# Moving both attention score blocks one gate tile later in a fused decoder layer

## The chip, the cores and the metric

The kernel runs on one core of one Trainium2 chip. The metric is the device time of one execution in microseconds. A core has a matrix engine (TensorE, "PE" in the profile), a vector engine (VectorE, "DVE"), a scalar engine (ScalarE, "ACT"), a general engine (GpSimd, "POOL") and a sync engine (SyncE, "SP") whose queue issues nearly all transfers here. Each engine takes its own instructions strictly in the order of the program, and waits where an operand isn't there yet.

## The reference

The layer maps x (256 tokens, 1024 features, float32) to an output of the same shape:

```
h = rmsnorm(x);  q, k, v, u_pool, gate_logits = split(h @ w_in)
q, k = rotary(rmsnorm(q)), rotary(rmsnorm(k))          # 8 heads of 64
attn = softmax(causal(q k^T / 8)) v
pooled = per-group map of (trailing mean over 2, 4, 8, 16 tokens - u_pool)
gates = sigmoid(gate_logits + b_gate)                  # 2 x 1024
x = x + (gates0 * (attn @ w_branch_attn) + gates1 * (pooled @ w_branch_pool)) @ w_out
up = conv3(rmsnorm(x) @ w_up)
out = x + (silu(up_gate) * up_value) @ w_down
```

With 256 tokens and blocks of 256, the block-sparse attention of the reference is plain causal attention over one block.

## The kernel before

Every product of two float32 matrices is made of three matmuls on split operands: a high part rounded on ACT (`high`, L91), a low part, the remainder, on DVE (`low`, L95 and L97), and then high x high, high x low and low x high on PE (`mm3`, L103 to L105). All weights come in blocks of 1 MB: a load on SP's queue (L132, tiles `raw_*`), then two halves of `high` (`hi_*`) and `low` (`lo_*`). A raw buffer is loaded again as soon as the low part of the block that was in it has been made, so the place of a load on SP's queue follows from the place of a `low` on DVE's queue.

The order of work is written out in the program. After q, k, v and the four pool groups come the 16 gate tiles, n = 0 to 15 (L649 to L681). A gate tile is 24 matmuls `ps_g<-xhi/xlo,hi_g/lo_g`; `chunk("g")` takes a new weight block at every even n. Between the tiles other work is placed by n: the last steps on the heads' q and k (`part_high`, `part_low`, which write tiles `qp` and `kp`), the scores, and at n = 12 the pool maps (`pool_maps`, PSUM tile `ps_m`), whose results are scaled two tick calls later by `pool_scaled` (`poolh` on ACT, `pooll` on DVE L97). `tick()` counts the tiles, and `later(m, f)` puts f after m more ticks.

The heads are dealt with in four pairs, two pairs at a time. For one such half `scores` makes 20 matmuls (L534) into the PSUM tiles `ps_s` of its two pairs (the pool `ps2` has two such buffers, and `ps_m` and the later `ps_o` use the same two). Then DVE adds the mask and takes the row maxima (L542 to L549), and ACT makes the exponentials (L562): those of the first pair at once, those of the second (`behind`) after the next gate tile. Then a block transposition on DVE (L280) and a store to HBM (`spill`, L284, `home_w<-y`) turn the weights of a pair; one tick after that four reads (`fill`, L292, `sm` or `y<-home_w`) bring them back. At the last pair the row sums go the same way: `home_sums` (L583, four small stores) and the broadcast reads `RS<-home_sums` (L590). The first pair's transposition is put down two ticks after its exponentials, that of the second goes through the list `held`, and is emitted at the end of a tile, after `ahead` has put down the next pieces of weight splitting.

After the 16 gate tiles comes the pool branch, eight feature blocks j (`ps_bp`, 12 matmuls each); with j = 4 the attention values of all pairs (`ps_o`, L600, 32 matmuls) are inserted. They are scaled by RS (L616), and split into the tile `heads` (ACT L91, DVE L95). The attention branch `ps_ba` follows with eight blocks, which need `heads`; then the output projection and the FFN, which take the rest of the time.

Of the kernel before, what the change touches and what calls it, by code (L numbers as in the profile page):

```python
# [70 lines left out]
def hybrid_layer_kernel(ctx: ExitStack, tc: tile.TileContext, xq_d, xtok_d, par_d, wkv_d, wpg_d,  # L71
# [70 lines left out]
    for c, (name, src) in enumerate(order):  # L142
        n = CH if name == "q" else src.shape[-1]
# [17 lines left out]
    def next_high():  # L161
        if at[0] < len(pieces):
            c, sl, first, _ = pieces[at[0]]
            if c - oldest() >= WBUFS:
                return
            at[0] += 1
            if first:
                moving = order[c][0] in "qkv"
                place = MOVING if moving else 0
                his[c] = whi_p.tile([P, CH + P], F32R, tag="whi", name=f"hi_{order[c][0]}{c}")[:, place:]  # L170
                place = MOVING if moving else FAR
                los[c] = wlo_p.tile([P, CH + P], F32R, tag="wlo", name=f"lo_{order[c][0]}{c}")[:, place:]
            high(his[c][:, sl], raw(c, sl))

    def next_low(eager=False):
        if at[1] < at[0] - STAGGER or at[0] == len(pieces) > at[1] or (at[1] < at[0] and eager):
            c, sl, _, last = pieces[at[1]]
            at[1] += 1
            low(los[c][:, sl], his[c][:, sl], raw(c, sl))
            if last:  # L180
                split.add(c)
                while loaded[0] - RAWBUFS in split and order[loaded[0] - RAWBUFS][0] != "q" and loaded[0] < len(order):
                    load()
# [3 lines left out]
    def ahead(upto=0):  # L187

        next_high()
        next_low()  # L190
        if at[1] - sum(p[0] < used[0] for p in pieces) < upto:
            next_high()
            next_low()

    def chunk(name):
        c = used[0]
        used[0] += 1
        spent.update(i for i in range(c) if order[i][0] != "dn")
        assert order[c][0] == name and all(p[0] != c or name == "dn" and p[3] for p in pieces[at[1]:]), (name, order[c][0])
        return his[c], los[c]  # L200
# [130 lines left out]
    def big(name):  # L331
        return tmp.tile([P, 2 * 2 * 3 * P], F32, tag="big", bufs=2, name=name)
# [90 lines left out]
    def tick():  # L423
        clock[0] += 1
        for fn, args in due.pop(clock[0], []):
            fn(*args)


    def feature_tile(w, c, name):
        hi, lo = w  # L430
        ps = bank(f"ps_{name}")
        for k in range(KD):
            sl = slice(k * 256 + c * P, k * 256 + (c + 1) * P)
            mm3(ps[:, 0:S], (hi[:, sl], lo[:, sl]), (xhi[:, k, :], xlo[:, k, :]), k == 0, k == KD - 1)
        return ps
# [61 lines left out]
    def part_high(name):  # L497
        for t in range(NT):
            high(part(name, 0, t), head_rows(name, t))

    def part_low(name):
        for t in range(NT):
            low(part(name, 1, t), part(name, 0, t), head_rows(name, t))
# [3 lines left out]
    def gate(n):  # L507
        return gates[:, n // 2, n % 2, :]
# [9 lines left out]
    def scores(hps):  # L518
        if not turned:
            sms, ys = big("sm0"), big("y0")  # L520
            turned.append(ys)
        else:
            sms = turned.pop()
            ys = act.tile([P, 2 * 2 * 3 * P], F32, tag="qk", name="y2")
        pss = []
        for hp in hps:
            pss.append(ps2.tile([P, 2, 512], F32, tag="ps2", name=f"ps_s{hp}"))
            for t, part, keys in ((1, 1, 0), (1, 0, 0), (1, 0, 1), (0, 0, None), (0, 1, 0)):
                for j in range(2):
                    rows = slice(j * DH, (j + 1) * DH)  # L530
                    out = pss[-1][:, j, TOK[t]]
                    if keys is None:
                        out = pss[-1][:, j, :].rearrange("p (a b) -> p a b", b=P)[:, 0:4:3, :]
                    nc.tensor.matmul(out, qp[rows, part, hp, t * P:(t + 1) * P],  # L534
                                     kp[rows, :, hp, 0:P] if keys is None else kp[rows, keys, hp, 0:(t + 1) * P],
                                     start=t == part == 1, stop=(t, part, keys) in ((1, 0, 1), (0, 1, 0)),
                                     skip_group_check=True)
        for i, (hp, ps) in enumerate(zip(hps, pss)):
            on = slice(i * 6 * P, (i + 1) * 6 * P)
            sm = sms[:, on].rearrange("p (j c) -> p j c", j=2)  # L540
            mx = tmp.tile([P, 2, 2], F32, tag="mx", name=f"mx{hp}")
            nc.vector.tensor_tensor(sm[:, :, TOK[0]], ps[:, :, 3 * P:4 * P],  # L542
                                    mask[:, 1:2, :].to_broadcast([P, 2, P]), ALU.add)
            for j in range(2):
                for t in (1, 0):
                    nc.vector.tensor_tensor_reduce(sm[:, j, TOK[t]], ps[:, j, TOK[t]],
                                                   whole if t else sm[:, j, TOK[0]], 1.0, LOWEST,
                                                   ALU.add, ALU.max, mx[:, t, j:j + 1])
            nc.vector.scalar_tensor_tensor(mx, mx, -1.0, qs[:, :, 2 * hp:2 * hp + 2], ALU.mult, ALU.mult)  # L549
            if i == 0:  # L550
                exponentials(hp, sm, mx, ys[:, on], sms[:, on])
            else:
                behind.append((exponentials, hp, sm, mx, ys[:, on], sms[:, on]))
# [4 lines left out]
    def exponentials(hp, sm, mx, *flat):  # L558
        for j in range(2):
            for t in (1, 0):  # L560
                at = j * H + NT * hp + t
                nc.scalar.activation(sm[:, j, TOK[t]], sm[:, j, TOK[t]], AF.Exp, bias=mx[:, t, j:j + 1],  # L562
                                     scale=qs[:, t, 2 * hp + j:2 * hp + j + 1], accum_out=rsum[:, at:at + 1])
        if hp % 2:
            later(1, held.append, (turn_weights, hp, *flat))
        else:
            later(2, turn_weights, hp, *flat)
# [57 lines left out]
    def sigmoids(n):  # L625
        for _ in range(min(n, len(waiting))):
            f = waiting.pop(0)
            nc.scalar.activation(gate(f), gate(f), AF.Sigmoid, bias=par[:, C_BG + f:C_BG + f + 1])

    def pool_maps():  # L630
        wph, wpl = chunk("pool")
        pm = ps2.tile([P, 2, 512], F32, tag="ps2", name="ps_m")
        for g in range(NG):
            sl = slice(g * P, (g + 1) * P)
            mm3(pm[:, g // 2, (g % 2) * S:(g % 2 + 1) * S], (wph[:, sl], wpl[:, sl]),
                (poolh[:, g, :], pooll[:, g, :]), True, True)
        for i in range(2):
            later(1 + i, pool_scaled, pm, (2 * i, 2 * i + 1))
# [10 lines left out]
    for n in range(2 * KD):  # L649
        if n == 1:  # L650
            for _ in range(2):
                next_high()
            for _ in range(2):
                next_low()
        if n in (2, 3):
            part_high("q" if n == 2 else "k")
        if n in (5, 10):
            scores((0, 1) if n == 5 else (2, 3))
        if n == 2 * MAPS:
            pool_maps()  # L660
            ahead()
        b, c = n // 2, n % 2
        if c == 0:
            w = chunk("g")
        ps = feature_tile(w, c, f"g{n}")
        tick()
        ahead(AHEAD if n % 2 else 0)
        for fn, *args in behind + held:
            fn(*args)
        behind.clear()  # L670
        held.clear()
        f = 2 * GATES[b] + c
        if n in PLAIN:
            nc.scalar.activation(gate(f), ps[:, 0:S], AF.Copy)
            plain.append(f)
        else:
            nc.vector.tensor_tensor(gate(f), ps[:, 0:S], R1, ALU.mult)
        if n in (2, 3):
            part_low("q" if n == 2 else "k")
        if n >= 2 * KD - 2:  # L680
            sigmoids(3)  # L681
# [295 lines left out]
```

## Time and profile before

| | us |
|---|---|
| median of three runs (lowest, highest) | 331.68 (329.95, 332.16) |
| the profiled execution, its own time | 329.45 |
| its span in the trace | 327.7 |
| PE busy in the span | 322.5 (98%) |
| DVE busy | 259.5 (79%) |
| ACT busy | 201.4 (61%) |
| first scores start on PE | 62.5 |
| second scores start on PE | 78.83 |
| attention values start on PE | 104.89 |
| attention branch starts on PE | 111.84 |

Times in the rows count from the start of the span. A row of the timeline has the start, the duration, the engine, the line, the operation and what it writes and reads; in brackets stands how long the engine sat idle just before it, and what ended that. Durations of neighbouring instructions overlap, since the engines are pipelined: what a step costs its engine is the difference between two starts. SPq rows are the issues on SP's queue, not the transfers; "DMA to landing" is the time from an issue until the data has landed.

### The profile page before, as it was taken

The numbers are of one execution on the slowest core, as the hardware profiler recorded it, in microseconds if no ns is written. First come the engines' busy times: TensorE is split into PE (matmuls) and PEld (weight loads), VectorE is DVE, ScalarE is ACT, GpSimd is POOL, SyncE is SP. The second block draws the span as 40 slices with busy tenths as digits, with TensorE's granted clock in tenths as the row PEclk, the third lists the DMA queues.
The fourth block names the chain that finished last, engine by engine and source line by source line (L and its number), as shares of the span: only waits on it lengthen the run. The fifth ranks groups of instructions, "written<-read, shape, count | busy, mean of one in ns | idle before, by whom it ended". The sixth has DMA issues, their size and how long they took to land.

```text
span 327.7 us, 6762 instructions
## 1 busy us (share of the span) xinstructions
PE 322.5 (98%) x2708; PEld 315.5 (96%) x2708; DVE 259.5 (79%) x447; ACT 201.4 (61%) x329; POOL 71.3 (22%) x89
## 2 busy tenths in 40 slices
PE   8999999899999999999999999999999999999996
PEld 8888899899999999999999999999999999999995
DVE  5839989998989866879997978686868686868844
ACT  5768609584995657668676746474647474746520
POOL 1006690000000051130421222212121212121330
PEclk9999999999999999999999999999999999999999
DMA  7999799748977933644627455454545454643003
GB/s 257 424 418 233 240 356 304 281 180 254 301 251 225 403 128 120 241 157 144 242 80 307 158 228 196 190 202 187 199 187 206 181 210 176 212 174 130 0 2 128
DMA packets 15710, 69.72 MB, mean 213 GB/s; under 512 B 2112, under 2 KB 6464, under 8 KB 8640
## 3 DMA queue, kind: packets, MB, share of 16 engines
q1 hardware_dynamic: 15264, 69.17, 59.6%
q8 instruction: 21, 0.34, 0.4%
q10 hardware_dynamic: 416, 0.13, 0.3%
q14 instruction: 9, 0.07, 0.1%
HBM read 65.61 MB, written 3.68 MB: 211 GB/s over the span
## 4 chain that ended last, share of the span: by engine, by line
PE 80%; DMA 12%; DVE 5%; issue 1%; ACT 1%; SPq 1%; DVEq 0%; ACTq 0%
PE ps_up L104 12%; PE ps_up L105 12%; PE ps_up L103 12%; PE ps_d L838 6%; PE ps_d L839 6%; PE ps_d L837 6%; DMA raw_v<-in_wkv 4%; PE ps_g L103 3%; PE ps_g L104 3%; PE ps_g L105 3%; DMA R<-rows 3%; PE ps_out L105 2%; PE ps_out L104 2%; PE ps_out L103 2%; DMA xq<-in_xq 2%; DMA home_k<-y_k 1%
## 5 line engine op out<-in xcount | busy, mean ns | idle before, releaser
L105 PE MATMUL ps_up<-hhi,lo_up 128*128 128x256 f32 x352 | 97.2, 276 | 0.0
L103 PE MATMUL ps_up<-hhi,hi_up 128*128 128x256 f32 x352 | 97.2, 276 | 0.0
L104 PE MATMUL ps_up<-hlo,hi_up 128*128 128x256 f32 x352 | 97.2, 276 | 0.0
L104 PEld LDWEIGHTS ps_up<-hlo,hi_up 128*128 128x128 f32 x352 | 66.1, 188 | 0.0
L105 PEld LDWEIGHTS ps_up<-hhi,lo_up 128*128 128x128 f32 x352 | 66.1, 188 | 0.0
L103 PEld LDWEIGHTS ps_up<-hhi,hi_up 128*128 128x128 f32 x352 | 66.1, 188 | 0.0
L95 DVE TENSOR_TENSOR lo_up<-raw_up,hi_up 128x1024 fp32r<-128x1024 f32 x44 | 54.7, 1262 | 7.3 <-ACT hi_up L91 7.3
L837 PE MATMUL ps_d<-ah,hi_dn 128*128 128x256 f32 x176 | 48.6, 276 | 0.0
L838 PE MATMUL ps_d<-al,hi_dn 128*128 128x256 f32 x176 | 48.6, 276 | 0.0
L839 PE MATMUL ps_d<-ah,lo_dn 128*128 128x256 f32 x176 | 48.6, 276 | 0.0
L91 ACT ACTIVATE hi_up<-raw_up 128x1024 fp32r<-128x1024 f32 x44 | 44.1, 1047 | 0.0
L819 POOL TENSOR_TENSOR c_v<-c_g,c_v 128x256 f32<-128x256 f32 x22 | 16.2, 737 | 121.5 <-DVE c_v L802 121.5
L91 ACT ACTIVATE ah<-c_v 128x256 fp32r<-128x256 f32 x22 | 9.2, 418 | 45.6 <-POOL c_v L819 45.6
L103 PE MATMUL ps_g<-xhi,hi_g 128*128 128x256 f32 x128 | 35.6, 278 | 0.0
L105 PE MATMUL ps_g<-xhi,lo_g 128*128 128x256 f32 x128 | 35.4, 277 | 0.0
L104 PE MATMUL ps_g<-xlo,hi_g 128*128 128x256 f32 x128 | 35.4, 276 | 0.0
L838 PEld LDWEIGHTS ps_d<-al,hi_dn 128*128 128x128 f32 x176 | 33.0, 188 | 0.0
L837 PEld LDWEIGHTS ps_d<-ah,hi_dn 128*128 128x128 f32 x176 | 33.0, 188 | 0.0
L839 PEld LDWEIGHTS ps_d<-ah,lo_dn 128*128 128x128 f32 x176 | 33.0, 188 | 0.0
L95 DVE TENSOR_TENSOR lo_dn<-raw_dn,hi_dn 128x1024 fp32r<-128x1024 f32 x22 | 27.8, 1264 | 0.4 <-ACT hi_dn L91 0.4
L807 DVE TENSOR_TENSOR u_v<-ps_up,R 128x256 f32<-128x256 f32 x22 | 9.3, 421 | 20.9 <-PE ps_up L105 20.8
L844 POOL TENSOR_TENSOR al<-c_v,ah 128x256 fp32r<-128x256 f32 x22 | 22.0, 1000 | 11.6 <-ACT ah L91 11.6
(196 smaller groups left out, 779.5 us busy)
## 6 DMA issues: line engine op xcount, KB each, us to landing
raw_up<-in_wup SPq DMA_DIRECT2D x22, 1024.0 KB, 4.9
raw_dn<-in_wdn SPq DMA_DIRECT2D x11, 1024.0 KB, 4.9
raw_g<-in_wpg SPq DMA_DIRECT2D x8, 1024.0 KB, 7.2
raw_o<-in_wout SPq DMA_DIRECT2D x4, 1024.0 KB, 9.0
raw_v<-in_wkv SPq DMA_DIRECT2D x2, 1024.0 KB, 15.5
raw_p<-in_wpg SPq DMA_DIRECT2D x2, 1024.0 KB, 12.9
raw_bp<-in_wbp SPq DMA_DIRECT2D x2, 1024.0 KB, 5.9
raw_ba<-in_wba SPq DMA_DIRECT2D x2, 1024.0 KB, 7.3
```

The source lines that it names most:

```text
L91: nc.scalar.activation(hi, src, AF.Copy, scale=scale)
L95: nc.vector.tensor_tensor(lo, src, hi.bitcast(F32), ALU.subtract)
L103: nc.tensor.matmul(out, sh, mh, start=start, stop=False, **kw)
L104: nc.tensor.matmul(out, sh, ml, start=False, stop=False, **kw)
L105: nc.tensor.matmul(out, sl, mh, start=False, stop=stop, **kw)
L807: nc.vector.tensor_tensor(u, ps[:, 0:S], R2, ALU.mult)
L819: nc.gpsimd.tensor_tensor(uc[1], g[1], uc[1], ALU.mult)
L837: nc.tensor.matmul(o, hi[:, sl], acch[i], start=first, stop=False, skip_group_check=True)
L838: nc.tensor.matmul(o, hi[:, sl], accl[i], start=False, stop=False, skip_group_check=True)
L839: nc.tensor.matmul(o, lo[:, sl], acch[i], start=False, stop=i == KF - 1, skip_group_check=True)
L844: nc.gpsimd.tensor_tensor(accl[i], act_i, acch[i].bitcast(F32), ALU.subtract)
```

## The change

The scores of pairs 0 and 1 are put ahead of gate tile 6 in place of tile 5, those of pairs 2 and 3 ahead of tile 11 in place of tile 10. The pool maps stay ahead of tile 12, and the attention values stay within the pool branch.

```
-        if n in (5, 10):
-            scores((0, 1) if n == 5 else (2, 3))
+        if n in (6, 11):
+            scores((0, 1) if n == 6 else (2, 3))
```

What `scores` sets off by ticks moves with it. On PE, around the first scores, the row before reads (ps_g_753 is gate tile 4, ps_g_827 tile 5, ps_s the score tiles of pairs 0 and 1):

```order
L105 MATMUL ps_g_753<-xhi,lo_g_643 128x256
L534 MATMUL ps_s_787<-kp,qp 128x256 x6
L534 MATMUL ps_s_787<-kp,qp 128x2x128 x2
L534 MATMUL ps_s_787<-kp,qp 128x128 x2
L534 MATMUL ps_s_798<-kp,qp 128x256 x6
L534 MATMUL ps_s_798<-kp,qp 128x2x128 x2
L534 MATMUL ps_s_798<-kp,qp 128x128 x2
L103 MATMUL ps_g_827<-xhi,hi_g_642 128x256
```

And in the changed kernel, where ps_g_785 is tile 5 and ps_g_855 tile 6:

```order
L105 MATMUL ps_g_785<-xhi,lo_g_643 128x256
L534 MATMUL ps_s_815<-kp,qp 128x256 x6
L534 MATMUL ps_s_815<-kp,qp 128x2x128 x2
L534 MATMUL ps_s_815<-kp,qp 128x128 x2
L534 MATMUL ps_s_826<-kp,qp 128x256 x6
L534 MATMUL ps_s_826<-kp,qp 128x2x128 x2
L534 MATMUL ps_s_826<-kp,qp 128x128 x2
L103 MATMUL ps_g_855<-xhi,hi_g_650 128x256
```

The 24 matmuls of tile 5 now stand ahead of the scores.

On DVE, after the second scores, the row before has the transposition of pair 3 (y_1018; the row shown first is the low part of the last gate block) ahead of the reciprocals of the sums and of the scaled pool maps (pooll):

```order
L95 TENSOR_TENSOR lo_g_1086<-raw_g_782,hi_g_1085 128x1024
L280 STREAM_TRANSPOSE y_1018<-y_786 128x6x4x32
L677 TENSOR_TENSOR xq<-ps_g_1096,R_169 128x256
L95 TENSOR_TENSOR lo_g_1086<-raw_g_782,hi_g_1085 128x1024
L578 RECIPROCAL rsum<-rsum 128x16
L580 STREAM_TRANSPOSE yr<-rsum 128x32
L97 SCALAR_TENSOR_TENSOR pooll<-ps_m,par,poolh 128x256 x2
L95 TENSOR_TENSOR lo_bp_1144<-raw_bp_897,hi_bp_1143 128x1024
```

In the changed kernel the place of that transposition (y_1051) and what stands ahead of it:

```order
L97 SCALAR_TENSOR_TENSOR pooll<-ps_m,par,poolh 128x256 x2
L95 TENSOR_TENSOR lo_bp_1138<-raw_bp_890,hi_bp_1137 128x1024
L280 STREAM_TRANSPOSE y_1051<-y_814 128x6x4x32
L677 TENSOR_TENSOR xq<-ps_g_1143,R_169 128x256
L97 SCALAR_TENSOR_TENSOR pooll<-ps_m,par,poolh 128x256 x2
L578 RECIPROCAL rsum<-rsum 128x16
L580 STREAM_TRANSPOSE yr<-rsum 128x32
L95 TENSOR_TENSOR lo_bp_1138<-raw_bp_890,hi_bp_1137 128x1024
```

It now stands behind the first two scaled pool maps and the first half of the pool branch's weights; the reciprocals follow later too.

On SP's queue, in the same stretch, one piece of the difference (raw_bp and raw_ba are loads of weights for the pool and attention branches, home_w the stores of pairs 2 and 3, y<-home_w the reads of pair 2):

```order
 L132 DMA raw_bp_980<-in_wbp 128x2048
-L132 DMA raw_ba_1089<-in_wba 128x2048
-L284 DMA home_w_1122<-y_1018 128x768
-L284 DMA home_w_1127<-y_1018 128x768
-L132 DMA raw_ba_1147<-in_wba 128x2048
-L292 DMA y_786<-home_w_1122 32x4x192 x4
+L132 DMA raw_ba_1048<-in_wba 128x2048
+L132 DMA raw_ba_1141<-in_wba 128x2048
+L284 DMA home_w_1169<-y_1051 128x768
+L284 DMA home_w_1178<-y_1051 128x768
+L292 DMA y_814<-home_w_1169 32x4x192 x4
 L583 DMA home_sums<-yr 16x32 x4
```

The second load of raw_ba, 1 MB, changes places with the two stores: it is issued ahead of them. In the first half, the second store of pairs 0 and 1 likewise comes to stand directly behind the first, with the load of raw_bp ahead of both.

## The prediction

> **What bounds the kernel now.** I read PE's own waits first, since PE is busy for 98% of the span. In the whole execution the list has one row beside the start of the program:
>
> ```profile
> PE ps_s L534 <- DVE kp L95: 0.9, 1, 0.9
> ```
>
> These are the first scores, which wait for the low part of k. So PE sets the time from there to the end, and a microsecond taken out of PE's row is worth a microsecond, until something that PE needs later comes too late. PE's timeline at the first scores, and at the second ones:
>
> ```profile
> 62.29 0.28 PE L105 MATMUL ps_g<-xhi,lo_g 128*128 128x256 f32 x1
> ...
> 63.89 1.16 PE L534 MATMUL ps_s<-kp,qp 64*128 64x256 f32 x16 [0.89 <-DVE kp L95]
> 64.98 0.39 PE L103 MATMUL ps_g<-xhi,hi_g 128*128 128x256 f32 x1
> ...
> 78.62 0.28 PE L105 MATMUL ps_g<-xhi,lo_g 128*128 128x256 f32 x1
> ...
> 80.15 0.38 PE L103 MATMUL ps_g<-xhi,hi_g 128*128 128x256 f32 x1
> ```
>
> From the last matmul of one gate tile to the first of the next it is 2.69 us at the first scores and 1.53 us at the second, where nothing is waited for. The wait with its restart costs 1.16 us.
>
> Then I looked for what is nearly late behind it. That is the attention branch, whose second matmul in every group of three reads the low parts of `heads`. PE at the values (ps_o) and there, and the rows of DVE and ACT that deliver them:
>
> ```profile
> 104.89 1.52 PE L600 MATMUL ps_o<-sm,vn 128*64 128x256 f32 x16
> ...
> 111.95 0.28 PE L104 MATMUL ps_ba<-heads,hi_ba 128*128 128x256 f32 x1
> ...
> 112.29 0.28 PE L104 MATMUL ps_ba<-heads,hi_ba 128*128 128x256 f32 x1
> ```
> ```profile
> 110.86 1.43 DVE L95 TENSOR_TENSOR heads<-RS,heads 128x256 fp32r<-128x256 f32 x4
> ```
> ```profile
> 107.96 1.06 ACT L91 ACTIVATE hi_o<-raw_o 128x1024 fp32r<-128x1024 f32 x1 [5.19 <-DMA raw_o<-in_wout]
> ```
>
> The four low pieces take 1.43 us and end at 112.29. The two rows of ps_ba are one group of three matmuls apart, 0.34 us; the fourth low piece is wanted three groups after 111.95, at 112.97. The margin is 0.68 us. And this DVE row doesn't hang on PE: ACT stood 5.19 us before it made hi_o, until the load raw_o landed, and the high parts of `heads` and DVE's lo_o stand behind hi_o. raw_o is issued on SP right behind the reads of the attention weights and sums. So the time at which SP is through with the weights of pairs 2 and 3 sets the earliest start of the attention branch, and has 0.68 us to spare.
>
> **The change part by part.**
>
> *The first scores, one tile later.* A tile is eight groups of 0.34 us, 2.72 us. PE would start the last matmul ahead of the scores at 62.29 + 2.72 = 65.0; kp was there by 63.89, where the waiting row starts. The wait goes: -1.16 us on PE. What comes in its place is not late: tile 5 uses the block whose first half tile 4 has just used. The masks and exponentials of pairs 0 and 1 move by about 1.6 us; their weights come back some 20 us before the values use them at 104.89, so I cost that at nothing.
>
> *The second scores.* They come 2.72 - 1.16 = 1.56 us later. The pool maps keep their place, one tile behind them where it was two, and need a PSUM buffer from the first of the two score tiles. DVE's rows of before, at the masks and behind them:
>
> ```profile
> 79.67 0.42 DVE L542 TENSOR_TENSOR y<-ps_s,mask 128x256 f32<-128x256 f32 x1 [0.95 <-PE ps_s L534]
> ...
> 82.96 0.42 DVE L95 TENSOR_TENSOR pooll<-pl,poolh 128x256 fp32r<-128x256 f32 x1
> 83.30 1.22 DVE L95 TENSOR_TENSOR lo_g<-raw_g,hi_g 128x1024 fp32r<-128x1024 f32 x1
> 84.43 0.42 DVE L677 TENSOR_TENSOR xq<-ps_g,R 128x256 f32<-128x256 f32 x1
> ...
> 86.83 0.98 DVE L280 STREAM_TRANSPOSE y<-y 128x768 f32<-128x768 f32 x1
> ```
>
> The masks of two pairs take 79.67 to 82.96, 3.29 us, and would run from 81.2 to 84.5. The first pair's half is over by 82.9; the pool maps come at 80.15 + 2 x 2.72 - 1.16 = 84.4. Covered, with 1.5 us to spare. If that cover goes, each microsecond that DVE is late beyond it stops PE.
>
> *The transposition of pair 3.* It is the costly step. ACT's rows:
>
> ```profile
> 81.49 0.60 ACT L562 ACTIVATE y<-y,mx,qs 128x256 f32<-128x256 f32 x1 [2.17 <-DVE mx L549]
> ...
> 83.63 1.05 ACT L91 ACTIVATE hi_g<-raw_g 128x1024 fp32r<-128x1024 f32 x1
> ...
> 88.60 0.81 ACT L91 ACTIVATE poolh<-ps_m,par 128x256 fp32r<-128x256 f32 x2
> ```
>
> In the new order ACT makes the exponentials of pair 2 (81.49 to 83.63, 2.14 us) from 83.05 to 85.2, half of hi_g (0.95) to 86.15, the exponentials of pair 3 (2.1) to 88.25, half of hi_bp (0.95) to 89.2, and then the scaled pool maps, the first done by 89.6. DVE makes the half of lo_g that needs that hi_g from 86.15 (1.13, from the starts 83.30 and 84.43) to 87.3, turns pair 2 (0.9) to 88.2, and then stands until 89.6 for poolh; two scaled maps (0.8) and half of lo_bp (1.13) follow, and only at 91.5 the transposition of pair 3, which was at 86.83. What is queued on DVE behind that wait of 1.4 us and the late transposition: an evacuation, two scaled maps, the reciprocals and the rest of lo_bp, some 2.7 us, to 95.1. PE wants it in the pool branch, whose five blocks ahead of the values (12 matmuls or 1.36 us each) start at 104.89 - 6.8 - 1.16 = 96.9. Covered by 1.8 us.
>
> *SP's queue.* Its issues before, and how long from issue to landing: the two stores at 85.8 and 87.8, and the two raw_ba loads, in that order (least, median, most).
>
> ```profile
> 84.54 0.35 SPq L132 DMA_DIRECT2D raw_ba<-in_wba  x1
> 85.76 2.40 SPq L284 DMA_DIRECT2D home_w<-y  x2
> 89.28 0.34 SPq L132 DMA_DIRECT2D raw_ba<-in_wba  x1
> 92.33 2.02 SPq L292 DMA_DIRECT2D y<-home_w  x4
> 94.46 2.95 SPq L583 DMA_DIRECT2D home_sums<-yr  x4
> 97.45 1.85 SPq L292 DMA_DIRECT2D y<-home_w  x4
> ```
> ```profile
> DMA to landing us min/median/max: 5.4/6.0/6.6
> DMA to landing us min/median/max: 6.7/7.3/7.8
> ```
> ```profile
> 84.00:88.00 4.00, 4.00 (x37) 4.00 (x37) 4.00 (x6) 4.00 (x11) 0.00 (x0) 1.00 0.97 350
> ```
> ```profile
> SPq L583 <- DMA raw_ba<-in_wba: 1.3, 1, 1.3
> ```
>
> Before, the reads of pair 2 went out when its store had landed (85.76 + 6.6 = 92.4), the DMA engines being full (0.97 at 350 GB/s in the window row). Now the store of pair 2 goes out at 88.3, behind both raw_ba loads. The late end: the second load, 1.05 MB at 350 GB/s, is 3.0 us more ahead of it, and it lands at 95.4. The early end: SP can't issue the reads before the store of pair 3, at 92.5 to 92.85, so 92.85 whatever the landing. Both raw_ba loads go out some 2 us earlier than before: the first hung on the lo_g half that ended at 84.43 and now stands ahead of the masks, the second now goes at 87.3 with the lo_g above. That pulls from the late end to the early one; I take the middle, 94.1. The reads take 2.13 us of SP (92.33 to 94.46). The sums took 2.99, of which 1.3 were a wait for the second raw_ba, which now lands earlier: 1.7. So the reads of pair 3 go out at 94.1 + 3.8 = 97.9 in place of 97.45, and RS and raw_o behind them likewise: 0.5 us later.
>
> One more gate stands there: in the new queue the fourth small store needs the transfer of pair 3's store finished. That store is issued at 92.5. By the nearest rows, 5.4 to 6.6 in a full queue, it lands at 97.9 to 99.1, and pair 3's reads then go out at up to 99.5, 2.05 us later than before. By the row of pair 0's store, the quickest of the four, it takes
>
> ```profile
> DMA to landing us min/median/max: 2.3/2.3/2.3
> ```
>
> and lands at 94.8, in time. It now stands behind the loads and no load behind it, so I take the quick row, and keep the slow one for the range. [...]
>
> *The sum.* With d for the shift of raw_o, `heads` is ready at its old time plus d, and PE wants it 1.16 us earlier with 0.68 to spare: the change is the larger of -1.16 and d - 0.68. With d = +0.5 it is -0.2 us; with the early end, d = 92.85 + 3.8 - 97.45 = -0.8, it is -1.16; with 95.4, d = +1.75, +1.1; with the late store of pair 3, +1.4. Behind the attention branch no row of PE waits, so the difference stays to the end: the profiled execution of 329.45 us (its span of 327.7 and 1.75 around it) would be 329.25, and the median 331.68 would be 331.5.
>
> **The rivals.**
>
> *The gain survives whole* (-1.16 us, 330.5): if the store of pair 2 lands by 93. For it speaks that the loads ahead of it are issued earlier; against it that the engines were full from 84 to 88, and 3.5 MB stand in the queue.
>
> *Slower, through pair 3's store.* Transposed 4.7 us later than before, it holds the sums and its own reads back. It decides from the point where they go out 0.7 us later than before, at 98.1; the price is +1.4 us (333.1) with the 6.6 us row. For +3 us the store would have to take 8.2 us, which no row of this stretch does.
>
> *PE stops at the pool maps* for the PSUM buffer: needs masks later by over 1.5 us. A microsecond beyond that leaves -0.2 us of the gain ahead of the branch, about 331.5 again; nothing in the rows speaks for it.
>
> *The change doesn't do what it says:* if kp came late again at 65.0, PE would still wait. kp has 1.1 us in hand and its chain isn't touched; with the whole wait back nothing is gained, and d = 0.5 is within the margin of 0.68: 331.7.
>
> **How the numbers follow.** No change to speak of (-0.7 to +0.7 us) 0.50; gain whole 0.20; slower through pair 3 0.22, a fifth of it beyond +3; pool maps 0.05; kp 0.03. The likeliest is 331.5 us (its own range 331.0 to 332.4). The known cases span 330.5 to 333.1; the three runs themselves lie 2.2 us apart, more than any case, so the range for 8 in 10 is 330.0 to 333.3. One per cent is 3.3 us, about what a measurement of this kernel can tell from no change. No case gains that much: 0.04, for the scatter of the runs alone. Slower by as much needs the long stall, 0.04, or the scatter, 0.02: 0.06. Within: 0.90.
>
> **What would show it.** Right: the wait of PE for kp is gone, the first scores take 1.5 us, the second start near 80.4; pair 3's transposition stands near 91.5 on DVE behind a wait for poolh; the reads of pair 3 go out near 98; a new wait of PE of about 1 us for the low part of `heads` at the attention branch, near 111.7, which gives back most of the gain. Wrong: no such wait (the store landed early), or a wait at ps_o or ps_m, or a wait for `heads` longer than 2 us.

## The result and the profile after

The changed kernel takes 333.82 us in the median of 22 runs (330.17 to 337.01); the kernel before, in 22 runs on the same chip, 330.38 us (329.01 to 332.21). The ratio is 1.0075, with a 95% interval of 1.0049 to 1.0101: slower, where no change was forecast, and outside the range. (The ratio leaves out runs over 1.5% above the fastest of their kernel, five of the changed kernel's; no trace of these five was kept, but an execution of 334.69 us further on, which falls to the same rule, has the same waits, so the ratio is probably too kind to the change.) The profiled execution took 333.92 us, its span is 332.1 us, 4.4 more than before.

PE's waits in the whole span of the changed kernel, but for the one at the start of the program:

```profile
PE ps_ba L103 <- ACT heads L91: 1.7, 1, 1.7
PE ps_ba L104 <- DVE heads L95: 1.2, 1, 1.2
```

The wait for `kp` is gone, and two others stand at the attention branch: one for the high part of `heads` and, one matmul later, one for the low part. PE's timeline at the two scores and there:

```profile
65.85 1.39 PE L534 MATMUL ps_s<-kp,qp 64*128 64x256 f32 x20
...
80.99 1.39 PE L534 MATMUL ps_s<-kp,qp 64*128 64x256 f32 x20
...
111.17 0.28 PE L105 MATMUL ps_bp<-poolh,lo_bp 128*128 128x256 f32 x1
113.10 0.38 PE L103 MATMUL ps_ba<-heads,hi_ba 128*128 128x256 f32 x1 [1.66 <-ACT heads L91]
114.66 0.39 PE L104 MATMUL ps_ba<-heads,hi_ba 128*128 128x256 f32 x1 [1.17 <-DVE heads L95]
...
115.59 0.42 PE L103 MATMUL ps_ba<-heads,hi_ba 128*128 128x256 f32 x1
115.81 0.41 PE L104 MATMUL ps_ba<-heads,hi_ba 128*128 128x256 f32 x1
```

The last two rows show a third thing: the matmuls behind the waits start 0.21 to 0.22 us apart, where neighbours in the rows of before are 0.11 to 0.12 apart. The windows of one microsecond (columns: time, PE, weight loads, DVE, ACT, POOL, then the granted clock, the DMA share and GB/s) say why:

```profile
114.00:115.00 1.00, 0.34 (x2) 0.34 (x3) 1.00 (x4) 1.00 (x2) 0.00 (x0) 1.00 0.99 418
115.00:116.00 1.00, 1.00 (x7) 1.00 (x6) 1.00 (x4) 1.00 (x3) 0.00 (x0) 0.53 0.97 410
116.00:117.00 1.00, 1.00 (x7) 1.00 (x6) 0.28 (x1) 0.52 (x2) 0.00 (x0) 0.50 0.74 311
...
118.00:119.00 1.00, 1.00 (x8) 1.00 (x8) 0.67 (x1) 0.00 (x0) 1.00 (x1) 0.76 0.00 0
```

From 115.1 to 118.5 the granted clock is 0.50. Of those 3.4 us half is lost, 1.7 us. The output projection starts (first `ps_out`) at 127.17, where it was 122.72. Without a wait the branch would start one matmul behind the row at 111.17, at 111.28: 127.17 - 111.28 = 15.9 us. Before, it was 122.72 - 111.84 = 10.9 us. So the attention branch costs 5.0 us more: 1.7 of clock, and 3.3 of waits with their restarts (111.28 to 113.10 and 113.21 to 114.66). The sum over the span: -1.2 for the wait for `kp`, +0.6 because this execution reached the first scores 0.6 us late for its own reasons (65.85, where 62.5 + 2.72 = 65.2 was due), +5.0 at the branch: 4.4.

### The profile page after: what moved, and what is told of

Its sections match the earlier page's. It is cut to its first block, busy times and chain, and to the rows that moved or that the text cites. A ratio compares the mean times of both kernels' runs of the same rounds, so it can differ in the third digit from the quotient of the medians.

```text
span 332.1 us, 6760 instructions
## 1 busy us (share of the span) xinstructions
PE 325.0 (98%) x2708; PEld 317.8 (96%) x2708; DVE 260.5 (78%) x447; ACT 201.4 (61%) x329; POOL 71.7 (22%) x89
## 4 chain that ended last, share of the span: by engine, by line
PE 93%; ACT 2%; DMA 2%; DVE 1%; issue 0%; ACTq 0%
PE ps_up L105 12%; PE ps_up L104 12%; PE ps_up L103 12%; PE ps_d L839 6%; PE ps_d L838 6%; PE ps_d L837 6%; PE ps_g L103 4%; PE ps_g L105 4%; PE ps_g L104 4%; PE ps_q L321 3%; PE ps_k L321 3%; PE ps_v L321 3%; DMA raw_o<-in_wout 2%; PE ps_out L105 2%; PE ps_out L104 2%; PE ps_out L103 2%
```

## The experiments

Each kernel ran beside the kernel before on the same chip, and the ratio is to that kernel. The granted clock of a whole run is a marker here. It came out as 1.000 to 0.998, as 0.995 or 0.993, or as 0.990 or 0.988, and one stretch like the above is 1.7 of 332 us, 0.005. So the clock gives an estimate of how many such stretches a run without a trace had: none, one or two. The three profiles with 0.995 show one stretch each; none at 0.990 was kept.

**The changed kernel once more.**

> The changed kernel itself, beside the next three on one chip. Every theory expects a median of 332.5 to 334 us against 329.5 to 330.5 of before, with a spread of several us among its own runs; runs of mean granted clock 0.995 stand some 1.7 us above those of 1.000.

Measured: 334.41 us (329.65 to 335.58, 11 runs), ratio 1.0062 [1.0020, 1.0104]. Nine of 11 runs are at 0.995 or below; the two at full clock took 329.65 and 330.32. In the first set six of 22 are at full clock, with a median of 331.0, and the ten at 0.995 have 333.8. The runs with the stretch stand further above the others than the 1.7 us that were expected, so the long waits and the half clock come together. PE's waits in its profile, and SP's queue:

```profile
PE ps_ba L103 <- ACT heads L91: 2.8, 1, 2.8
PE ps_ba L104 <- DVE heads L95: 1.2, 1, 1.2
```
```profile
88.71 4.91 SPq L284 DMA_DIRECT2D home_w<-y  x2
97.63 2.86 SPq L292 DMA_DIRECT2D y<-home_w  x4
```

The store of pair 2 leaves at 88.71 and the reads behind it go out at 97.63, 8.9 us later; in the first profile of the same program it was 6.0 us. So the link that the prediction priced with one number is a spread: executions of one program differ by some 3 us there.

**Only the first scores later.**

```diff
-        if n in (6, 11):
+        if n in (6, 10):
```

> Only the first scores are moved (n = 6), the second stay at n = 10. My theory after the result: the first move by itself is good, and everything lost comes from the second block, whose weights come back later while PE is 1.16 us ahead. Then PE's wait for kp is gone, the second scores start 1.2 us earlier than before, raw_o lands no later than before (d between -1.2 and 0), PE waits at most 0.5 us for heads, and the kernel is 0.5 to 1.2 us faster than before (ratio 0.996 to 0.9985). The rival, that the new order of SP's queue in the first half (the raw_bp load ahead of both stores) is what delays the loads behind it: then raw_o lands 1 us or more later than before, there is a wait of over 1 us for heads, and the kernel is slower than before.

Measured: 330.45 us (12 runs) against 329.93, ratio 0.9998 [0.9969, 1.0028]. The wait for `kp` is gone here too, and yet nothing is gained. Its only wait behind the start of the program, and ACT at raw_o:

```profile
PE ps_ba L104 <- DVE heads L95: 1.0, 1, 1.0
```
```profile
108.86 1.06 ACT L91 ACTIVATE hi_o<-raw_o 128x1024 fp32r<-128x1024 f32 x1 [6.75 <-DMA raw_o<-in_wout]
```

PE comes 0.9 us earlier to the branch, hi_o stands 0.9 us later (107.96 before), and the wait moves from `kp` to `heads`. The order of SP's queue around the second scores is here that of before. The expected 0.5 us of wait at most, and the gain, were wrong; but the named rival, the new order of the first half, isn't shown either: raw_o and the wait lie at its threshold of 1 us, and the kernel isn't slower.

**Only the second scores later** (against the kernel before).

```diff
-        if n in (5, 10):
+        if n in (5, 11):
```

> Only the second scores are moved (n = 11), the first stay at n = 5 with their wait. My theory: the wait for kp is back, PE is 1.16 us later at the attention branch than in the changed kernel, and the weights of pairs 2 and 3 are 1.2 us later still, so heads comes about 1.2 us later and PE waits about as long for it as in the changed kernel (2.5 to 3.5 us), with half clock behind the wait; 3 to 5 us slower than before (ratio 1.008 to 1.015), at least as slow as the changed kernel. The rival, that the loss comes from the first half: no wait for heads over 0.5 us, and the time of before.

Measured: 332.13 us (330.35 to 333.86, 12 runs) against 329.93, ratio 1.0062 [1.0037, 1.0087]. Its waits:

```profile
PE ps_ba L103 <- ACT heads L91: 1.4, 1, 1.4
PE ps_s L534 <- ACT kp L91: 1.4, 1, 1.4
PE ps_ba L104 <- DVE heads L95: 1.2, 1, 1.2
...
PE ps_s L534 <- DVE kp L95: 0.3, 1, 0.3
```

The loss is here: about 2 us, and nothing from the first scores. It is less than the 3 to 5 us that were expected, and the interval takes in the ratio of the changed kernel. It also shows that the clock is only a part of it: nine of the 12 runs are at full clock, the profiled one too, which at 333.86 us is the slowest of them. The wait for `kp`, in place as before, is 1.4 + 0.3 us in this execution, 0.9 in the profile of before and 0.4 in another below, so that gain too was a spread.

**Pair 3's store earlier** (the rival). The scaled pool maps are put one tick later, so that pair 3's transposition no longer stands behind them on DVE:

```diff
-            later(1 + i, pool_scaled, pm, (2 * i, 2 * i + 1))
+            later(2 + i, pool_scaled, pm, (2 * i, 2 * i + 1))
```

> The changed kernel with the scaled pool maps one tick later, so that the transposition and the store of pair 3 come about 2 us earlier (near 90.5 in place of 92.5) and DVE no longer stands 1.7 us for poolh. The prediction's rival that pair 3's late store holds the sums and its reads: then raw_o and heads come 1 to 2 us earlier and the kernel is 1.5 us or more faster than the changed one. My theory now, that the store of pair 2, behind both raw_ba loads, is what the reads wait for: raw_o lands at its old time within 0.5 us, and the time is that of the changed kernel within 0.7 us.

Measured: 332.77 us (330.13 to 334.77, 12 runs), ratio 1.0061 [1.0028, 1.0095]. The transposition starts at 90.64 in place of 92.54. Pair 2's reads on SP's queue, and what PE waits for:

```profile
94.67 2.03 SPq L292 DMA_DIRECT2D y<-home_w  x4
```
```profile
PE ps_ba L104 <- DVE heads L95: 1.2, 1, 1.2
...
PE ps_ba L103 <- ACT heads L91: 1.0, 1, 1.0
```

Both waits are still there, and eight of 12 runs have the half-clock stretch: pair 2's reads go out at 94.67, where the changed kernel has 94.94, since they hang on pair 2's own store. Pair 3's store isn't the gate in these profiles: it has landed at 95.6 here and at 95.8 in the changed kernel, ahead of the sums on SP's queue at 96.80 and 97.14. What the edit is worth stays open. raw_o is in at 110.26, 1.0 us ahead of the changed kernel's first profile, and the median is 1.6 us below that of the changed kernel beside it, the price that the rival had named; but the runs of the two overlap, and so do the ratios (1.0061 and 1.0062).

**Transpositions and stores of pairs 2 and 3 earlier.** With hp > 1 the exponentials put down the transposition one tick later themselves, in place of passing it through `held`, and pair 2's reads are put down two ticks later instead of one, so that they keep their place:

```diff
-        if hp % 2:
+        if hp > 1:
+            later(1, turn_weights, hp, *flat)
+        elif hp % 2:
             later(1, held.append, (turn_weights, hp, *flat))
...
-        later(1, fill_weights, hp, spill(y, f"w{hp}"), sm)
+        later(2 if hp == 2 else 1, fill_weights, hp, spill(y, f"w{hp}"), sm)
```

> The changed kernel with the transpositions of pairs 2 and 3 put down one tick earlier each, so that the store of pair 2 goes out near 87 ahead of the second raw_ba load, and that of pair 3 near 90. My theory, that the place of pair 2's store on SP's queue is the cause: its reads go out 1.5 to 2.5 us earlier than in the changed kernel, raw_o lands that much earlier, the wait for heads falls from about 3 us to under 1.5, the clock stays 1.00, and the kernel is 2 to 4 us faster than the changed one, within 0.7 us of before. The rival, that the weights are late because the scores are (the chain from masks to reads just starts 1.6 us later, whatever the order of the queue): raw_o no more than 0.7 us earlier, and at most 1 us faster than the changed kernel.

Measured: 331.24 us (329.43 to 334.15, 12 runs), ratio 1.0033 [0.9996, 1.0069]. The median is 3.2 us below that of the changed kernel beside it; the intervals of the two ratios overlap. Five of 12 runs still have the half-clock stretch. SP's queue, and what it waited for:

```profile
87.04 0.33 SPq L284 DMA_DIRECT2D home_w<-y  x1
89.61 0.33 SPq L132 DMA_DIRECT2D raw_ba<-in_wba  x1
...
92.19 2.21 SPq L292 DMA_DIRECT2D y<-home_w  x4
94.51 5.13 SPq L585 DMA_DIRECT2D home_sums<-yr  x4
```
```profile
SPq L585 <- DMA raw_ba<-in_wba: 2.8, 1, 2.8
```

The store of pair 2 is ahead of the second raw_ba load again and its reads go out at 92.19, as before the change. Now the sums wait 2.8 us for that load, which had landed in time in the changed kernel. So the place of this store on SP's queue is where much of the delay comes from, and moving it passes part of the delay on to the next gate. Whether the order counts, or only that the store goes out 1.9 us earlier than the 88.96 of the changed kernel, this edit doesn't tell, since it moves both.

**The idle time filled.** Sixteen matmuls that nothing reads (into a spare PSUM tile) stand ahead of the attention branch, in a row of 2.08 us on PE. They add work and take none away; only the idle stretch becomes shorter:

```diff
+    spare = bank("ps_spare")
+    for i in range(16):
+        nc.tensor.matmul(spare[:, 0:S], xhi[:, i % KD, 0:P], xhi[:, i % KD, :], start=True, stop=True)
```

> The changed kernel with 16 matmuls of 256 columns, of whose result nothing is used, on PE ahead of the attention branch: they take 16 x 0.1133 = 1.8 us and lie wholly within the wait for heads of 3.3 us. It measures the clock by itself: heads comes at the same time, so without a clock effect the time is that of the changed kernel (within 0.3 us). If half clock behind the wait is a cost of its own, the granted clock stays 1.00 at the attention branch, and the kernel is 1.5 to 1.9 us faster than the changed kernel (334 to about 332), still slower than before.

Measured: 332.32 us (332.07 to 335.08, 6 runs) against 329.93, ratio 1.0097 [1.0059, 1.0135]; four of six runs are at full clock, the profiled one too. PE there:

```profile
113.29 0.35 PE L103 MATMUL ps_ba<-heads,hi_ba 128*128 128x256 f32 x1
114.59 0.40 PE L104 MATMUL ps_ba<-heads,hi_ba 128*128 128x256 f32 x1 [0.95 <-DVE heads L95]
```

The second matmul starts at 114.59, as in the changed kernel (114.66), since `heads` is just as late. But the output projection starts at 125.49 in place of 127.17: 1.7 us, the price of the half clock by itself, seen in one profile each. Over all runs the ratio is not better than the changed kernel's, where 1.5 to 1.9 us were expected, and two of the six still have the stretch; so few runs say no more.

**The link cut, first form.** The two pieces of weight splitting for the output projection that ACT and DVE had ahead of `heads` (hi_o and lo_o among them) are put behind it; the rest is the changed kernel:

```diff
             tick()
-            ahead()
-        if j in (0, 2, 4, 6):
+            if j != VALUES + 1:
+                ahead()
+        if j in (0, 2, 6):
             ahead()
...
                 rests(hps)
+            ahead()
+            ahead()
```

> The changed kernel, in which the two steps of weight splitting that stand ahead of the split of heads (blocks j = 4 and 5 of the pool branch) are put behind it, so that neither ACT's high parts of heads nor DVE's low parts stand behind the load raw_o. My theory, that raw_o is the link: the high parts of heads follow the values at once (near 108 to 109), PE doesn't wait at the attention branch at all (under 0.3 us), the granted clock stays 1.00, and the whole 1.16 us are kept: 0.8 to 1.4 us faster than before (ratio 0.996 to 0.998), some 3.5 to 4 us faster than the changed kernel. The rival, that the late weights themselves (reads of pair 3, RS) hold the values: a wait at ps_o or at RS in its place, heads not before 111, and a time within 1 us of the changed kernel.

Measured: 330.38 us (329.24 to 331.95, 12 runs) against 329.93, ratio 1.0013 [0.9991, 1.0034], no run below full clock. The waits:

```profile
PE ps_ba L103 <- DVE xq L705: 1.2, 1, 1.2
PE ps_ba L104 <- DVE heads L95: 0.2, 1, 0.2
```

The expected gain didn't come. The waits for `heads` fall from 2.8 to 0.2 us, and a new one is of the edit's own making: the moved splits now stand on DVE ahead of the evacuations (`xq`) that free the PSUM banks for `ps_ba`.

**The link cut, second form.** The splits go behind those evacuations too. Five kernels have this edit: with the scores of the changed kernel, with those of the kernel before, with the first scores alone moved, and the first and the third of these once more with the earlier transpositions of above.

```diff
             tick()
-            ahead()
-        if j in (0, 2, 4, 6):
+            if j < VALUES:
+                ahead()
+        if j in (0, 2):
             ahead()
...
                 rests(hps)
+        if j > VALUES + 1:
+            ahead()
```

> The changed kernel with the weight splitting of the output projection (hi_o, lo_o) put behind the split of heads and behind the evacuations of the last pool blocks. Theory (raw_o holds heads back through hi_o and lo_o on the in-order queues, and the two waits also cost a stretch of half clock): heads now hangs on RS and the values alone. PE's waits for heads shrink from 1.7 + 1.2 us to at most 1 us in sum, the granted clock stays at 1.00 in most runs, and the median is 3 us below the changed kernel, within 1 us of the kernel before. Rival (the sums and RS themselves come too late, raw_o only stands behind them): the wait for the high part of heads stays above 1.5 us, the time stays over 332 us.

Measured: 329.83 us (328.82 to 332.04, 12 runs) against 330.18, ratio 0.9994 [0.9969, 1.0020]; no run below full clock. In the profiled execution PE waits 0.3 and 0.2 us at the branch, and raw_o is no longer among the causes:

```profile
PE ps_ba L103 <- DVE xq L728: 0.3, 1, 0.3
...
PE ps_ba L104 <- DVE heads L95: 0.2, 1, 0.2
```
```profile
109.15 1.41 ACT L91 ACTIVATE heads<-RS 128x256 fp32r<-128x256 f32 x4 [4.38 <-DVE RS L616]
111.27 1.04 ACT L91 ACTIVATE hi_o<-raw_o 128x1024 fp32r<-128x1024 f32 x1
```

SP's queue is as late here as in the changed kernel (pair 2's reads at 97.11, raw_o issued at 105.21), and it no longer matters. The same delay without the link costs nothing that can be measured: the changed kernel's loss is this link. The gain of 1.16 us doesn't show either.

> The kernel before with the same edit of the weight splitting, scores where they were. Theory: its margin at the attention branch was not used up, so nothing is gained on the profiled execution, and the wait for kp (about 0.9 us) stays: same as before, within 0.3 us in the median, ratio 0.998 to 1.001, perhaps with less scatter. Rival (the edit is a gain of its own that has nothing to do with the place of the scores): as fast as the kernel with the first scores later and the same edit, ratio 0.995 to 0.998.

Measured: 329.77 us (329.52 to 330.34, 12 runs), ratio 0.9981 [0.9960, 1.0002]. The wait for `kp` stays, at 0.4 us in this profile, and it is the only one behind the first microseconds. Whether the edit gains by itself isn't settled by this interval; what is plain is the scatter, 0.8 us in 12 runs where the kernel before has 6.7 in 35 (329.17 to 335.82). Beside it the kernel with both scores moved has 329.83: with the link cut, moving them costs nothing that these runs show.

> First scores one tile later, second scores where they were, weight splitting behind heads, and the transpositions and stores of pairs 2 and 3 one tile earlier. Theory: without the link the attention branch has margin already, so the earlier stores buy nothing: ratio 0.996 to 0.998, no wait of PE after the start. Rival (RS still decides in many executions): another 0.3 us or more below the kernel without the earlier stores, 0.993 to 0.995.

Measured: 329.44 us (328.87 to 330.29, 12 runs), ratio 0.9979 [0.9955, 1.0003], no wait of PE behind its start. With the first scores alone moved, the earlier stores buy nothing that shows once the link is cut: without them, in the last kernel below, the ratio is 0.9969.

> The changed kernel with both remedies: weight splitting behind heads, transpositions and stores of pairs 2 and 3 one tile earlier. Theory: each takes away a part of the delay (the stores about 2.5 us at raw_o and RS, the splitting what is left), so that the gain of the missing wait for kp survives: no wait of PE above 0.3 us, clock 1.00, ratio 0.996 to 0.999. Rival (the later second scores cost PE something beside this chain): ratio above 1.000 with no wait for heads.

Measured: 329.16 us (328.86 to 330.74, 12 runs), ratio 0.9968 [0.9945, 0.9991]: faster than the kernel before, by 0.3%. Nothing waits in PE's row but the start. It is 0.7 us below the kernel with the same scores and without the earlier stores (329.83), and the intervals overlap: whether the stores buy something here isn't settled.

> Only the first scores are moved, and the weight splitting of the output projection is put behind the split of heads and the last evacuations of the pool branch. In the run with the first move alone PE waited 1.0 us for the low part of heads, behind raw_o, and nothing was gained. My theory, that this link alone gave the gain back: no wait of PE for heads (under 0.2 us), and 0.8 to 1.3 us faster than before (ratio 0.996 to 0.998), the fastest of all kernels here. The rival, that the late weights themselves hold heads: RS not landed when the values are done, a wait of 0.5 us or more at the attention branch, and no gain.

The first scores alone are moved and the link is cut. Measured: 329.26 us (328.78 to 329.80, 12 runs) against 330.62, ratio 0.9969 [0.9949, 0.9990], no run below full clock. ACT in its profile, and all that PE waits for:

```profile
107.67 1.41 ACT L91 ACTIVATE heads<-RS 128x256 fp32r<-128x256 f32 x4 [4.04 <-DVE RS L616]
110.30 1.07 ACT L91 ACTIVATE hi_o<-raw_o 128x1024 fp32r<-128x1024 f32 x1 [0.42 <-DMA raw_o<-in_wout]
```
```profile
PE ps_warm L236 <- DVE ones L204: 1.1, 1, 1.1
```

hi_o stands at 110.30, later than before (107.96), and the high parts of `heads` are made ahead of it. The ratio is worth 1.0 us of 330.6. That this is the 1.16 us of the missing wait for `kp` isn't shown: the fastest runs of the two kernels are alike (328.78 and 328.85), and the profiled span is 327.5 where it was 327.7. PE starts the output projection at 121.78, 0.94 us earlier than before, and loses 0.7 again in its first groups, where weight loads wait for a low part on DVE (`ml`). That wait is in the profiles of all six kernels with the cut and not in that of before; it is a price of the cut:

```profile
PEld ps_out L104 <- DVE ml L95: 0.6, 2, 0.3
```

By these rows, what the medians gain is in large part that the late runs are gone. With both forms of the cut, 72 runs in all by six kernels, no run fell below full clock. This kernel and the one ahead of it are faster than the kernel before and the changed one; between the two, and against the cut alone, the intervals don't decide.

## Why the prediction was wrong, point by point

*The first scores* were right: no wait for `kp`, one row of 20 matmuls. *The second scores and the masks* were right: scores at 80.99 where 80.4 was named (the 0.6 us is this execution's late start), masks from 81.84 to 85.1, no stop at the pool maps. *The transposition of pair 3* was right in its mechanism and near in size. DVE's rows:

```profile
87.96 0.97 DVE L280 STREAM_TRANSPOSE y<-y 128x768 f32<-128x768 f32 x1
90.62 0.88 DVE L97 SCALAR_TENSOR_TENSOR pooll<-ps_m,par,poolh 128x256 fp32r<-128x256 f32 x2 [1.68 <-ACT poolh L91]
...
92.54 0.97 DVE L280 STREAM_TRANSPOSE y<-y 128x768 f32<-128x768 f32 x1
```

The wait for `poolh` is 1.68 us (1.4 forecast), the transposition at 92.54 (91.5). *Pair 3's store* lands 2.3 us after its issue, the quick row that was taken, and isn't the gate. That was partly luck: in the second profile of the same program it took 5.3 us, and where 8.2 us was called beyond every row, it took 8.6 in the kernel with the earlier transpositions. SP's queue and the two stores (least, median, most from issue to landing):

```profile
88.96 4.91 SPq L284 DMA_DIRECT2D home_w<-y  x2
94.94 2.10 SPq L292 DMA_DIRECT2D y<-home_w  x4
97.14 3.04 SPq L583 DMA_DIRECT2D home_sums<-yr  x4
100.28 1.80 SPq L292 DMA_DIRECT2D y<-home_w  x4
102.26 1.14 SPq L590 DMA_DIRECT2D RS<-home_sums  x2
103.49 3.45 SPq L132 DMA_DIRECT2D raw_o<-in_wout  x4
```
```profile
DMA to landing us min/median/max: 2.3/4.1/6.0
```

*The gain given back at the attention branch* by raw_o, hi_o and `heads` was the right mechanism: ACT made hi_o at 111.29, when raw_o had landed, and DVE then had lo_o ahead of the low part of `heads`:

```profile
111.29 1.06 ACT L91 ACTIVATE hi_o<-raw_o 128x1024 fp32r<-128x1024 f32 x1 [7.75 <-DMA raw_o<-in_wout]
...
112.65 1.32 ACT L91 ACTIVATE heads<-RS 128x256 fp32r<-128x256 f32 x4
```
```profile
112.38 1.23 DVE L95 TENSOR_TENSOR lo_o<-raw_o,hi_o 128x1024 fp32r<-128x1024 f32 x1 [3.62 <-ACT hi_o L91]
...
114.19 1.43 DVE L95 TENSOR_TENSOR heads<-RS,heads 128x256 fp32r<-128x256 f32 x4
```

The step that failed is the size of d, the shift of raw_o. It was put at 0.5 us; hi_o went from 107.96 to 111.29, 3.3 us, or 2.7 without the execution's own 0.6. Set against the forecast, the 2.2 us between are: store and reads of pair 2, 94.94 + 2.20 where 94.1 + 2.13 and 0.6 were due, +0.3; the sums, 3.1 us of SP's time (97.14 to 100.28) where 1.7 was taken, +1.4; the reads of pair 3 and RS, 3.2 us (100.28 to 103.49) where they took 3.85 before (97.45 to 101.30), -0.6; the landing of raw_o, 7.8 us behind its issue (103.49 to 111.29) where it was 6.7 (101.30 to 107.96), +1.1. No wait of SP for the sums is left, as forecast; one of the four small issues (98.48) took 1.70 us by itself. In the second profile of the changed kernel one of pair 2's reads took 1.16 us to issue. Before, the long issue was one of RS (99.48, 1.09 us), so part of the +1.4 and of the -0.6 is one thing at two places. In the two profiles of these sums a transfer of the queue that the profile names "q8 instruction" (0.02 MB) starts within half a microsecond of the long issue, between 98.4 and 98.5 here, between 99.1 and 99.2 before. That the transfer holds the issue up wasn't tested. The longer landing of raw_o stays unexplained.

With d = 2.7 the rule of the prediction, d - 0.68, gives +2.0 us, and the span less the 0.6 and the clock's 1.7 is 2.1 longer. In the second profile of the changed kernel hi_o starts at 112.28 and the first scores are 0.4 us late: d = 3.9, the rule gives +3.3, and the span of 332.9 less 0.4 and 1.7 is 3.1 longer. The rule holds, and its input was wrong. It was worked out for the low parts of `heads` alone; the wait for the high parts, which stand behind the same hi_o, wasn't forecast.

Behind this stands a choice that was wrong in kind: d came from one profile as if each landing had one value. The store of pair 2 took 6.0 and 8.9 us in two profiles of the changed kernel, and 6.6 and 7.5 us in those of the kernel before and of the one with the first scores alone moved. A shift that puts this store behind two loads of 1 MB has a long side and a short one of little more than a microsecond: the early end of the range was cut off by pair 3's transposition at 92.85, while the late end was taken from the mean rate of the engines (95.4). 97.6 occurred. In the first profile this store cost only 0.3 us of the 2.2; in the second it decided.

The term that was missing, put at nothing without a reason, is the clock, 1.7 us in most runs of the changed kernel. The rival with the right sign, "slower through pair 3's store", had the wrong gate and less than half the price (+1.4 us, where the medians are 3.4 apart), and its chance of 0.22 was mostly put within one per cent. What was named as showing the forecast wrong, a wait for `heads` of over 2 us, is what came: 2.8 in two pieces.

## What to carry to other kernels

When a wait is taken out ahead of a step with a margin of well under a microsecond, price that margin against the spread of the landings it hangs on, not against one profile; and look at what stands on the in-order queues ahead of the late step without being needed for it. Here moving two pieces of weight splitting behind `heads` made the kernel deaf to three microseconds of lateness, at a price of up to 0.7 us at the output projection. And a wait on TensorE can have a second price: here, behind 1.66 and 1.17 us of waiting, 3.4 us of half clock, which cost 1.7 us.

## What the runs showed of the hardware

Two waits of 1.66 and 1.17 us with a single matmul between them were followed by 3.4 us at a granted clock of 0.50. In the second profile of the changed kernel and in that with pair 3's store earlier the stretch is at 0.50 too and as long: from the clocks of the windows at its ends (0.60 and 0.69 in the one, 0.83 and 0.96 in the other) it runs from 115.2 to 118.6 and from 114.7 to 118.1. The idle time on PE there differs. From the end of the last matmul of the pool branch to the end of the waits, with one matmul in between, it was 3.2 us in the first profile (111.45 to 114.66), 4.3 in the second (111.32 to 115.64), and 2.6 in that with pair 3's store earlier (111.05 to 113.64). With the second scores alone moved it was 3.0 us (113.23 to 116.20), and the clock stayed at 1.00. So the length of the idle time doesn't by itself decide whether the stretch comes, nor do the single waits: 2.8 + 1.2 us and 1.0 + 1.2 us came with it in their profiles, 1.4 + 1.2 us without. What decides it these runs don't show. By the clocks of the runs it came in 25 of the changed kernel's 33, in five of the 99 of the kernel before beside the experiments, in none of the 72 with the link cut.

The store of pair 2, 384 KB on SP's queue, took 5.0 to 9.2 us to land in the fourteen profiles, that of pair 3 2.3 to 8.6 us in ten of them. In the changed kernel's first profile the DMA engines were at a share of 0.96 from 84 to 88 us, ahead of pair 2's store (6.0 us), and at 0.56 from 94 to 96, when pair 3's was under way (2.3 us). What sets the landing from execution to execution of one program stays open. So does the cause of the long issue on SP's queue, up to 1.70 us among neighbours of 0.4; the trace shows only what runs at the same time.
